# A four-layer decoder trunk on one core: scaled activations and split weights at staggered SBUF addresses, and two gate/up tiles multiplied in pieces

## The chip, the core and the metric

One core of one Trainium2 chip runs the whole trunk in one launch. The metric is the device time of that core in microseconds (us), taken as the median over runs. The host only permutes and joins the arrays that it is given.

## What is computed

Two layers of a macaron block. Each adds half a SwiGLU feed-forward, then a mixer (differential attention in layer 0, a chunked gating MLP in layer 1), then half of another feed-forward. All of it is float32.

```python
D_MODEL = 1024; SEQ = 512; D_FF = 2816
def _swiglu_ffn(x, w_gate_up, w_down):
    g, u = jnp.split(x @ w_gate_up, 2, axis=-1)
    return (jax.nn.silu(g) * u) @ w_down
def reference(...):
    for i in range(2):
        x = x + 0.5 * _swiglu_ffn(_rmsnorm(x, ffn1_norm[i]), ffn1_w_gate_up[i], ffn1_w_down[i])
        h = _rmsnorm(x, mix_norm[i])
        x = x + (_diff_attention(h, ...) if i == 0 else _chunked_sgu(h, ...))
        x = x + 0.5 * _swiglu_ffn(_rmsnorm(x, ffn2_norm[i]), ffn2_w_gate_up[i], ffn2_w_down[i])
    return x
```

## The kernel before

The residual lies on chip as eight tiles `x[k]`, 128 features by 512 tokens each. A product of float32 operands is made of three products of float32r operands (a float32 format that TensorE multiplies in one pass): each operand is split into a high part and the remainder, and `mm3` (lines 126 to 129) adds high times high, high times low and low times high in PSUM. One such matmul has 128 stationary columns (a piece of one operand, 512 bytes of each partition) and 512 moving columns (2048 bytes of each partition of the other operand). The TensorE row of a trace that belongs to it is MATMUL; the load of its stationary part is a LDWEIGHTS on the row PEld. The load for the next matmul starts when the present matmul starts.

- **Scaled x.** `Norm.halves` (lines 156 to 159) writes x times gain as `xh[k]` on ScalarE and its remainder `xl[k]` on VectorE, eight tiles of 2048 bytes each.
- **Weights.** `load` (line 113) brings up to 2048 columns into a raw tile through the SP queue; `split` (lines 118 to 124) makes a high and a low tile of up to 1024 columns from a part of it, out of a pool of five buffers for each. Weights are split ahead of their use.
- **Feed-forward** (`ffn`, f0 to f3, in the order of the trunk). 22 gate/up tiles of 48 matmuls: the weights are stationary and `xh`/`xl` move; then 16 down tiles of 33 matmuls: weights stationary, hidden tiles `hh`/`hl` moving. Each half of the hidden width does 11 gate/up tiles and 8 down tiles. f0 is the first of layer 0, f1 the second of layer 0. Down products are called `f0dp` to `f3dp` in rows, gate/up products `f0p` to `f3p`.
- **Attention** (`qk`, `v`, `aop` in rows) and **gating MLP** (`gv`, `gup`, `gs`, `gop`). In their input products (`qk`, `v`, `gv`) a piece of `xh`/`xl` is stationary and the weights move. `interleave` (line 311) emits the tasks of a mixer in the order of a rough clock. In the gating MLP: `v_block` (the columns mixed over tokens, `gv`), `layer_norm` and `affine` (four pairs of VectorE operations for each block of 512 columns, lines 692 and 693), `u_tile` (24 matmuls each, `gup`, kept in tiles `gut`), `mix` (four float32 matmuls, `gs`, line 707, that need the block's affine), and `out_part` (`gop`, with the mixed tiles `gh`/`gl` moving). `U_BUFS = 4` is the number of `gut` buffers, and u tile c is emitted only after mix c - U_BUFS.

Where the operands stand in SBUF, in bytes within a partition, as the built program places them (the trace does not show addresses):

```text
operand                          first byte      spacing   remainder by 512
xh[k], xl[k]                     36960           2048      96
split weights (pieces of 512 B)  69728 onwards   512       96
hidden tiles hh, hl              137440          2048      224
mixed tiles gh, gl               193152          2048      128
```

So in all products of x with weights, and in the attention's output product, the moving tile and the stationary piece begin at the same remainder by 512 bytes. In the down products they differ by 128 bytes, in the gating MLP's output products by 32.

Of the kernel before, what the change touches and what calls it, by code (L numbers as in the profile page):

```python
# [10 lines left out]
F32R = mybir.dt.float32r  # L11
# [6 lines left out]
P = 128  # L18
S = 512
NT = S // P  # L20
D = 1024
KT = D // P
# [22 lines left out]
O_BUFS = 4  # L45
U_BUFS = 4
QK_BUFS = 5
BANKS = {"pp": 4, "ps": 3, "po": 1}
HOP = 0.2
END = "end"  # L50


@with_exitstack
def kernel(
# [18 lines left out]
):  # L73
    """Activations stay on chip. The residual is kept feature-major, x[d, token]; float32 operands
    of the large products are split exactly into a float32r part and its float32r remainder, and
    hi*hi + hi*lo + lo*hi accumulate in PSUM. The RMS factor of a token is applied where a
    product leaves PSUM, so that products start on x*gain before it is known."""
    nc = tc.nc

    const = ctx.enter_context(tc.tile_pool(name="const", bufs=1))  # L80
    acts = ctx.enter_context(tc.tile_pool(name="acts", bufs=1))
    wraw = ctx.enter_context(tc.tile_pool(name="wraw", bufs=2))
    wsplit = ctx.enter_context(tc.tile_pool(name="wsplit", bufs=5))
# [7 lines left out]
    x = [acts.tile([P, S], F32, name=f"x{k}") for k in range(KT)]  # L91
    xh = [acts.tile([P, S], F32R, name=f"xh{k}") for k in range(KT)]
    xl = [acts.tile([P, S], F32R, name=f"xl{k}") for k in range(KT)]
    ident = const.tile([P, P], F32, name="ident")
# [16 lines left out]

# [1 line left out]
    def load(src, n, name):  # L113
# [4 lines left out]
    def split(raw, lo, n, name):  # L118
        """Exact float32r halves of n columns of raw."""
        wh = wsplit.tile([P, 1024], F32R, tag="wh", name=name + "h")  # L120
        wl = wsplit.tile([P, 1024], F32R, tag="wl", name=name + "l")
        nc.scalar.activation(wh[:, :n], raw[:, lo:lo + n], AF.Copy)
        nc.vector.tensor_tensor(wl[:, :n], raw[:, lo:lo + n], f32(wh[:, :n]), op=ALU.subtract)
        return wh, wl

    def mm3(ps, sh, sl, mh, ml, start, stop):
        nc.tensor.matmul(ps, sh, mh, start=start, stop=False)  # L127
        nc.tensor.matmul(ps, sh, ml, start=False, stop=False)  # L128
        nc.tensor.matmul(ps, sl, mh, start=False, stop=stop)  # L129

    def rsqrt(v, n, name):
        """v ** -0.5 of a [P, n] tile, to float32 rounding."""
        y = stat.tile([P, n], F32, tag=f"rs_y{n}", name=name + "y")
        t = stat.tile([P, n], F32, tag=f"rs_t{n}", name=name + "t")
        nc.vector.tensor_scalar(
            y.bitcast(I32), v.bitcast(I32), -0.5, RSQRT_MAGIC, op0=ALU.mult, op1=ALU.add
        )
        for _ in range(3):
            nc.vector.tensor_tensor(t, y, y, op=ALU.mult)
            nc.vector.scalar_tensor_tensor(t, t, -0.5, v, op0=ALU.mult, op1=ALU.mult)  # L140
            nc.vector.scalar_tensor_tensor(y, t, 1.5, y, op0=ALU.add, op1=ALU.mult)
        return y

    class Norm:
        """Collects x*gain and the sum of squares of a new residual, tile by tile."""

# [22 lines left out]
        def rstd(self):  # L169
            """[token, token tile] of 1/rms."""  # L170
            ps = bank(self.name + "ss", "po")
            for n in range(NT):
                nc.tensor.matmul(
                    ps[:, n:n + 1], self.acc[:, n * P:(n + 1) * P], ones[:, 0:1], start=True, stop=True
                )
            v = stat.tile([P, NT], F32, tag="rs_v4", name=self.name + "v")
            nc.vector.tensor_scalar(v, ps[:, :NT], 1.0 / D, RMS_EPS, op0=ALU.mult, op1=ALU.add)
            return rsqrt(v, NT, self.name)

        def rows(self, r):  # L180
            """[any partition, token] of 1/rms."""
            rh = stat.tile([P, NT], F32R, tag="rh", name=self.name + "rh")
            rl = stat.tile([P, NT], F32, tag="rl", name=self.name + "rl")
            nc.vector.tensor_scalar(rh, r, 1.0, None, op0=ALU.mult)
            nc.vector.tensor_tensor(rl, r, f32(rh), op=ALU.subtract)
            ps = bank(self.name + "rb", "po")
            for part, half in ((f32(rh), "h"), (rl, "l")):
                dg = stat.tile([P, NT, P], F32R, tag="sq", name=f"{self.name}dg{half}")
                nc.vector.tensor_tensor(
                    dg,  # L190
                    ident.unsqueeze(1).broadcast_to([P, NT, P]),
                    part.unsqueeze(2).broadcast_to([P, NT, P]),
                    op=ALU.mult,
                )
                nc.tensor.matmul(
                    ps, ones_r, dg.rearrange("p a b -> p (a b)"), start=(half == "h"), stop=(half == "l")
                )
            rb = stat.tile([P, S], F32, tag="rb", name=self.name + "rbs", bufs=1)
            nc.scalar.activation(rb, ps, AF.Copy)
            return rb  # L200

    def begin(norm):
        """Loads of x and of the first weights, in the order of their use, and their halves."""
        raw = wraw.tile([P, 2048], F32, tag="raw", name="w0")
        cuts = [(0, 1), (1, 2), (2, 4), (4, 6), (6, 8)]
        for a, b in cuts:
# [3 lines left out]
        nc.sync.dma_start(sm[:, C_BOUT:], small[:, C_BOUT:])  # L210
        parts = [
            [wsplit.tile([P, 1024], F32R, tag=t, name=f"w0{q}{t}") for t in ("wh", "wl")] for q in range(2)
        ]
        for a, b in cuts:
# [11 lines left out]
    def ffn(layer, which, norm, nxt):  # L226
        f = layer * 2 + which
        nm = f"f{f}"
        with ExitStack() as c:
# [19 lines left out]
            for half in range(2):  # L249
                hh, hl, late = [], [], []  # L250
                for jj in range(FH):
# [7 lines left out]
                    for k in range(KT):  # L259
                        wh, wl = parts[k // 4]  # L260
                        for u in range(2):
                            c0 = slice((k % 4 * 2 + u) * P, (k % 4 * 2 + u + 1) * P)
                            mm3(ps[u], wh[:, c0], wl[:, c0], xh[k], xl[k], k == 0, k == KT - 1)
                        if rb is None and jj == first:
                            if k == 3:
                                r = norm.rstd()
                            elif k == KT - 1:
                                rb = norm.rows(r)
# [23 lines left out]
    class Weights:  # L292
        """Pieces of 1024 columns of weights in the order of their use, two to a load, split ahead of it."""

# [16 lines left out]
    def interleave(tasks):  # L311
        """Emits tasks in the order of a rough clock of the engines. A task is (name, names of the
        tasks whose results it needs, or "<" and names of those that it only follows, generator); the
        generator yields (products' share, shares of the engines that take up the result one after the
        other, whether it waits for them or until when, or END); the earlier in the list, the higher
        its priority."""
        done, state, sent, now = {}, {}, {}, 0.0
# [36 lines left out]
    def project(weights, p, nm, norm, rr, taken):  # L354
        """[token, 512 columns] of x*gain against four pieces, p on, of weights; taken() emits what
        takes a token tile out of PSUM and returns the engines' shares."""
        ps = [bank(f"{nm}p{n}", "pp") for n in range(NT)]
# [21 lines left out]
    def attention(norm, nxt):  # L379
        with ExitStack() as c:  # L380
            a2 = c.enter_context(tc.tile_pool(name="a2", bufs=2, reuse_waits="tile"))

            # k gain * q gain / sqrt(d) on k; (1 - lambda_init) * subln gain; -lambda
            kg = const.tile([P, 1], F32, name="kg")
# [27 lines left out]
            def qk_block(hp):  # L412
                """q and k of two heads."""
                nm = f"qk{hp}"
# [12 lines left out]
            def v_block(b):  # L427
                """v of four heads."""
                vts[b] = a2.tile([P, NT, 512], F32, tag="vt", name=f"vt{b}", bufs=2)
# [48 lines left out]
            def scores(h, i):  # L478
                """Both softmaxes of query tile i, each before its division, and their difference."""
                hp, hh, nm = h // 2, h % 2, f"a{h}"  # L480
# [133 lines left out]
    def gmlp(norm, nxt):  # L614
        with ExitStack() as c:
# [34 lines left out]
            def v_block(b):  # L650
                """gelu of the 512 columns that are mixed over tokens."""
                br = row(b_in, 4 + b, "bin")
# [10 lines left out]
            def u_tile(c):  # L663
                """gelu of a tile of gates, [column, token]."""
                if "rb" not in rr:
# [30 lines left out]
            def mix(c):  # L696
                """Mixes a tile of v over the tokens of each chunk, [column, token], and gates it."""
                b, j, g = c // 4, c % 4, c // 2
# [60 lines left out]

# [1 line left out]
    nc.sync.dma_start(sm[:, :C_BOUT], small[:, :C_BOUT])  # L761
# [84 lines left out]
```

## Time and profile before

| | |
|---|---|
| time, median of 2 runs | 2024.37 us (2024.16 and 2024.58) |
| span of the profiled execution | 2022.6 us; the runs' time lies 1.8 us above it |
| TensorE matmul / weight load | 2012.6 us (100%) / 1627.5 us (80%) |
| VectorE / ScalarE / GpSimd | 1026.9 us (51%) / 670.4 us (33%) / 2.6 us |
| DMA | 190.33 MB, 26.7% of 16 engines for the data queue |
| granted TensorE clock, mean | 1.000 |

Busy times of matmuls overlap, since one starts while the one before it drains. The distance between the starts of neighbouring matmuls, called the pitch below, is what a matmul costs, and not its duration of 0.39 us. A row of the timeline has the start, the duration, the engine, the line, and output<-inputs.

### The profile page before, as it was taken

What the parts mean: (1) busy time and instruction counts of PE and PEld (TensorE: products, weight loads), DVE (VectorE), ACT (ScalarE), POOL (GpSimd) and SP (SyncE); (2) the same over time, 40 slices, a digit from 0 to 9 for tenths busy, and PEclk for the clock granted to TensorE, in tenths of its full rate; (3) what the DMA queues carried; (4) which work ended last, traced back from release to release, by engine and by line L of the source; (5) the groups of instructions that cost most, each with busy time, mean ns of one, the idle gap of its engine ahead of it and who ended that gap; (6) DMA issues with size and microseconds to landing.
All of it is one profiled execution on the core that took longest, in us unless ns stands there. A gap on an engine that the chain in (4) does not pass through costs nothing.

```text
span 2022.6 us, 22047 instructions
## 1 busy us (share of the span) xinstructions
PE 2012.6 (100%) x8970; PEld 1627.5 (80%) x8970; DVE 1026.9 (51%) x1647; ACT 670.4 (33%) x960; POOL 2.6 (0%) x11
## 2 busy tenths in 40 slices
PE   8999999999999999999999999999999999999999
PEld 7888888876668888888888888888888888888887
DVE  7433444556768543444454334444596564434442
ACT  5322323355554322232332223233332243222321
POOL 0000000000000000000000000000000000000000
PEclk9999999999999999999999999999999999999999
DMA  5223222211111222222322232224332222223222
GB/s 190 98 72 124 92 85 93 105 63 63 42 63 64 105 85 92 105 104 72 108 102 91 78 115 102 79 99 146 115 115 84 85 103 85 84 93 124 84 80 77
DMA packets 32933, 190.33 MB, mean 94 GB/s; under 512 B 3776, under 2 KB 4160, under 8 KB 16576
## 3 DMA queue, kind: packets, MB, share of 16 engines
q1 hardware_dynamic: 32832, 188.93, 26.7%
q8 instruction: 70, 1.15, 0.2%
q14 instruction: 31, 0.25, 0.0%
HBM read 186.82 MB, written 2.10 MB: 93 GB/s over the span
## 4 chain that ended last, share of the span: by engine, by line
PE 99%; DVE 0%; DMA 0%; ACT 0%; SPq 0%; issue 0%
PE f3p L127 4%; PE f2p L127 4%; PE f2p L128 4%; PE f3p L128 4%; PE f2p L129 4%; PE f3p L129 4%; PE f1p L128 4%; PE f1p L129 4%; PE f1p L127 4%; PE f0p L127 4%; PE f0p L129 4%; PE f0p L128 4%; PE f1dp L129 2%; PE f0dp L127 2%; PE f1dp L128 2%; PE f0dp L128 2%
## 5 line engine op out<-in xcount | busy, mean ns | idle before, releaser
L235 DVE TENSOR_TENSOR f3g<-f3p,n5rbs 128x512 f32<-128x512 f32 x22 | 15.2, 691 | 58.7 <-PE f3p L129 58.7
L235 DVE TENSOR_TENSOR f2g<-f2p,n3rbs 128x512 f32<-128x512 f32 x22 | 15.2, 691 | 58.7 <-PE f2p L129 58.7
L235 DVE TENSOR_TENSOR f1g<-f1p,n2rbs 128x512 f32<-128x512 f32 x22 | 15.2, 692 | 58.7 <-PE f1p L129 57.3
L235 DVE TENSOR_TENSOR f0g<-f0p,n0rbs 128x512 f32<-128x512 f32 x22 | 15.2, 691 | 55.5 <-PE f0p L129 55.5
L158 ACT ACTIVATE xh<-x,sm 128x512 fp32r<-128x512 f32 x48 | 34.3, 718 | 18.0 <-DVE x L737 9.5
L159 DVE SCALAR_TENSOR_TENSOR xl<-x,sm,xh 128x512 fp32r<-128x512 f32 x48 | 35.6, 746 | 8.6 <-ACT xh L158 8.5
L285 DVE SCALAR_TENSOR_TENSOR x<-f3dp,x 128x512 f32<-128x512 f32 x16 | 11.1, 692 | 42.3 <-PE f3dp L129 42.3
L491 PEld LDWEIGHTS <-ident_b 128*128 128x128 bf16 x64 | 6.1, 95 | 28.1 <-issue 26.2
L285 DVE SCALAR_TENSOR_TENSOR x<-f1dp,x 128x512 f32<-128x512 f32 x16 | 11.1, 692 | 31.0 <-PE f1dp L129 31.0
L285 DVE SCALAR_TENSOR_TENSOR x<-f2dp,x 128x512 f32<-128x512 f32 x16 | 11.1, 692 | 31.0 <-PE f2dp L129 31.0
L285 DVE SCALAR_TENSOR_TENSOR x<-f0dp,x 128x512 f32<-128x512 f32 x16 | 11.1, 692 | 31.0 <-PE f0dp L129 31.0
L737 DVE TENSOR_TENSOR x<-gop,x 128x512 f32<-128x512 f32 x24 | 16.5, 689 | 19.8 <-PE gop L129 19.8
L242 ACT ACTIVATE f3hh<-f3u 128x512 fp32r<-128x512 f32 x22 | 13.9, 632 | 28.0 <-DVE f3u L239 28.0
L242 ACT ACTIVATE f2hh<-f2u 128x512 fp32r<-128x512 f32 x22 | 13.9, 632 | 28.0 <-DVE f2u L239 28.0
L243 DVE TENSOR_TENSOR f3hl<-f3u,f3hh 128x512 fp32r<-128x512 f32 x22 | 15.2, 693 | 15.4 <-ACT f3hh L242 15.4
L243 DVE TENSOR_TENSOR f2hl<-f2u,f2hh 128x512 fp32r<-128x512 f32 x22 | 15.2, 693 | 15.4 <-ACT f2hh L242 15.4
L242 ACT ACTIVATE f1hh<-f1u 128x512 fp32r<-128x512 f32 x22 | 13.9, 631 | 27.2 <-DVE f1u L239 27.2
L580 DVE TENSOR_TENSOR x<-aop,x 128x512 f32<-128x512 f32 x32 | 21.4, 684 | 2.8 <-PE aop L129 2.7
L243 DVE TENSOR_TENSOR f1hl<-f1u,f1hh 128x512 fp32r<-128x512 f32 x22 | 15.2, 692 | 14.7 <-ACT f1hh L242 14.7
L242 ACT ACTIVATE f0hh<-f0u 128x512 fp32r<-128x512 f32 x22 | 13.9, 632 | 26.4 <-DVE f0u L239 26.4
L243 DVE TENSOR_TENSOR f0hl<-f0u,f0hh 128x512 fp32r<-128x512 f32 x22 | 15.2, 692 | 14.1 <-ACT f0hh L242 14.0
L717 ACT ACTIVATE gh<-gut 128x512 fp32r<-128x512 f32 x16 | 10.1, 631 | 33.8 <-DVE gut L716 33.8
(3603 smaller groups left out, 6451.7 us busy)
## 6 DMA issues: line engine op xcount, KB each, us to landing
f1gu<-in_gate_up_dram SPq DMA_DIRECT2D x22, 1024.0 KB, 4.8
f2gu<-in_gate_up_dram SPq DMA_DIRECT2D x22, 1024.0 KB, 4.7
f3gu<-in_gate_up_dram SPq DMA_DIRECT2D x22, 1024.0 KB, 4.8
f0gu<-in_gate_up_dram SPq DMA_DIRECT2D x21, 1024.0 KB, 4.8
f0d<-in_down_dram SPq DMA_DIRECT2D x16, 704.0 KB, 4.0
f1d<-in_down_dram SPq DMA_DIRECT2D x16, 704.0 KB, 4.1
f2d<-in_down_dram SPq DMA_DIRECT2D x16, 704.0 KB, 4.0
f3d<-in_down_dram SPq DMA_DIRECT2D x16, 704.0 KB, 4.0
```

Of the source, the lines that this page charges most:

```text
L127: nc.tensor.matmul(ps, sh, mh, start=start, stop=False)
L128: nc.tensor.matmul(ps, sh, ml, start=False, stop=False)
L129: nc.tensor.matmul(ps, sl, mh, start=False, stop=stop)
L158: nc.scalar.activation(xh[k], x[k], AF.Copy, scale=g)
L159: nc.vector.scalar_tensor_tensor(xl[k], x[k], g, f32(xh[k]), op0=ALU.mult, op1=ALU.subtract)
L235: nc.vector.tensor_tensor(gt, ps[0], rb, op=ALU.mult)
L242: nc.scalar.activation(a, ut, AF.Copy)
L243: nc.vector.tensor_tensor(b, ut, f32(a), op=ALU.subtract)
L285: nc.vector.scalar_tensor_tensor(x[m], pt, 0.5, x[m], op0=ALU.mult, op1=ALU.add)
L580: nc.vector.tensor_tensor(x[m], pt, x[m], op=ALU.add)
L717: nc.scalar.activation(gh, ut, AF.Copy)
L737: nc.vector.tensor_tensor(x[m], pt, x[m], op=ALU.add)
```

## The change

Three things. First, `xh[k]`, `xl[k]` and each split tile get 192 bytes more, and the operand begins at 0 to 6 steps of 32 bytes inside its tile: k mod 7 steps for `xh[k]`, 3k+4 mod 7 for `xl[k]`, and for the q-th pair of split tiles q mod 7 and 3q + q//8 mod 7. Second, to make room, `U_BUFS` is 2. Third, in f1 the gate/up tiles 3 and 5 take their moving operand in two pieces of 256 columns and four pieces of 128 columns, and the stationary part is loaded anew for each matmul of a piece.

```diff
-U_BUFS = 4
+U_BUFS = 2
+SHIFT = 8
+PAD = 6 * SHIFT
...
-    xh = [acts.tile([P, S], F32R, name=f"xh{k}") for k in range(KT)]
-    xl = [acts.tile([P, S], F32R, name=f"xl{k}") for k in range(KT)]
+    def shifted(pool, n, at, name, **kw):
+        o = at % 7 * SHIFT
+        return pool.tile([P, n + PAD], F32R, name=name, **kw)[:, o:o + n]
+    xh = [shifted(acts, S, k, f"xh{k}") for k in range(KT)]
+    xl = [shifted(acts, S, 3 * k + 4, f"xl{k}") for k in range(KT)]
+    places = iter(range(1 << 20))
+    def halves_of(name):
+        q = next(places)
+        return shifted(wsplit, 1024, q, name + "h", tag="wh"), shifted(wsplit, 1024, 3 * q + q // 8, name + "l", tag="wl")
...
-        wh = wsplit.tile([P, 1024], F32R, tag="wh", name=name + "h")
-        wl = wsplit.tile([P, 1024], F32R, tag="wl", name=name + "l")
+        wh, wl = halves_of(name)
...
-    def mm3(ps, sh, sl, mh, ml, start, stop):
+    def mm3(ps, sh, sl, mh, ml, start, stop, cuts=1):
+        if cuts > 1:
+            n = S // cuts
+            for a in range(0, S, n):
+                c = slice(a, a + n)
+                nc.tensor.matmul(ps[:, c], sh, mh[:, c], start=start and a == 0, stop=False)
+                nc.tensor.matmul(ps[:, c], sh, ml[:, c], start=False, stop=False)
+                nc.tensor.matmul(ps[:, c], sl, mh[:, c], start=False, stop=stop and a + n == S)
+            return
...
-                            mm3(ps[u], wh[:, c0], wl[:, c0], xh[k], xl[k], k == 0, k == KT - 1)
+                            cuts = {(1, 3): 2, (1, 5): 4}.get((f, j), 1)
+                            mm3(ps[u], wh[:, c0], wl[:, c0], xh[k], xl[k], k == 0, k == KT - 1, cuts)
```

In the built program after it `xh[k]` stands 2240 bytes apart, the split tiles 4288 bytes apart, and the shift comes on top. The hidden tiles begin at remainder 96 and the mixed tiles at 0. The remainder by 256 of (moving minus next stationary) then takes all eight multiples of 32 about equally often: among f1's 1248 gate/up matmuls each of the eight comes 124 to 170 times, among its 528 down matmuls 27 to 88 times.

On TensorE the first place is f1's gate/up tile 3 (`f1w30h` and `f1w30l` are the high and low parts of its first weights; `f1p_5349` and `f1p_5350` are the gate and the up accumulator). Before:

```order
L127 MATMUL f1p_5349<-xh_82,f1w30h 128x512
L128 MATMUL f1p_5349<-xl_90,f1w30h 128x512
L129 MATMUL f1p_5349<-xh_82,f1w30l 128x512
L127 MATMUL f1p_5350<-xh_82,f1w30h 128x512
L128 MATMUL f1p_5350<-xl_90,f1w30h 128x512
L129 MATMUL f1p_5350<-xh_82,f1w30l 128x512
```

With the change, the three rows of each accumulator come twice with 256 columns (shown once here):

```order
L144 MATMUL f1p_5349<-xh_82,f1w30h 128x256
L145 MATMUL f1p_5349<-xl_90,f1w30h 128x256
L146 MATMUL f1p_5349<-xh_82,f1w30l 128x256
...
L144 MATMUL f1p_5350<-xh_82,f1w30h 128x256
L145 MATMUL f1p_5350<-xl_90,f1w30h 128x256
L146 MATMUL f1p_5350<-xh_82,f1w30l 128x256
```

Tile 5 reads the same with four groups of 128x128. TensorE has 8858 rows where it had 8666: 48 more in tile 3, 144 more in tile 5.

On TensorE the second place is the first mix of the gating MLP (`gup` is the product of a u tile, `gs` that of a mix, and `gv_9780` to `gv_9783` are the four token tiles that `affine` finishes on VectorE). Before, the mixes of the first block come after all of u tile 3:

```order
L127 MATMUL gup_10494<-xh_89,gu2s1h 128x512
L128 MATMUL gup_10494<-xl_97,gu2s1h 128x512
L129 MATMUL gup_10494<-xh_89,gu2s1l 128x512
L707 MATMUL gs_10530<-wT,gv_9780 128x128
L707 MATMUL gs_10530<-wT,gv_9781 128x128
```

With the change (the token tiles are now `gv_9972` on) two mixes stand within u tile 2, after 13 of its matmuls:

```order
L150 MATMUL gup_10682<-xh_85,gu2s0l 128x512
L148 MATMUL gup_10682<-xh_86,gu2s0h 128x512
L727 MATMUL gs_10656<-wT,gv_9972 128x128
L727 MATMUL gs_10666<-wT,gv_9972 128x128
L149 MATMUL gup_10682<-xl_94,gu2s0h 128x512
L727 MATMUL gs_10656<-wT,gv_9973 128x128
L727 MATMUL gs_10666<-wT,gv_9973 128x128
L150 MATMUL gup_10682<-xh_86,gu2s0l 128x512
```

So 61 matmuls of u tiles stand ahead of the first mix, where there were 96.

On VectorE, at the same place, the first affine operation that a mix needs (line 693 before, line 713 now) stood right behind the rows of the next block:

```order
L692 SCALAR_TENSOR_TENSOR gv_9782<-gv_9782,lnmv,lng_10570 128x512
L693 SCALAR_TENSOR_TENSOR gv_9780<-gv_9780,lny,lnb_10452 128x512
L676 TENSOR_TENSOR gut_10447<-gup_10422,n4rbs 128x512
L693 SCALAR_TENSOR_TENSOR gv_9781<-gv_9781,lny,lnb_10452 128x512
```

With the change the take-up of u tile 1 and a split of weights stand ahead of it:

```order
L696 TENSOR_TENSOR gut_10639<-gup_10614,n4rbs 128x512
L162 SCALAR_TENSOR_TENSOR lny<-lnt,lny 128x4
L136 TENSOR_TENSOR gu6s0l<-gu6r,gu6s0h 128x1024
L713 SCALAR_TENSOR_TENSOR gv_9972<-gv_9972,lny,lnb_10644 128x512
L713 SCALAR_TENSOR_TENSOR gv_9973<-gv_9973,lny,lnb_10644 128x512
```

In the rest of the gating MLP mixes, u tiles and the loads and splits between them shift in the same manner, on SP, ScalarE, VectorE and TensorE; the mixes come in 17 groups on TensorE, where there were 9. Outside it the order of the engines is the same, but for one pair of neighbours on VectorE and ScalarE behind tile 5 of f1.

## Rows read from the trace of the kernel before

**Rows 1.** The page: busy time by engine, granted clock, the chain by engine.
```profile
PE 2012.6 (100%) x8970; PEld 1627.5 (80%) x8970; DVE 1026.9 (51%) x1647; ACT 670.4 (33%) x960; POOL 2.6 (0%) x11
...
PEclk9999999999999999999999999999999999999999
...
PE 99%; DVE 0%; DMA 0%; ACT 0%; SPq 0%; issue 0%
```

**Rows 2.** Waits of TensorE: us in total, times, longest us.
```profile
PE f0p L127 <- ACT w00wh L218: 5.8, 2, 5.2
PE f0p L127 <- ACT f0w10h L122: 0.2, 1, 0.2
PE n2rb L195 <- DVE n2dgh L189: 0.2, 1, 0.2
```

**Rows 3.** Timeline of PE in f1's gate/up tiles, first and last of 51.
```profile
899.62 0.39 PE L127 MATMUL f1p<-xh,f1w170h 128*128 128x512 f32 x1
899.85 0.39 PE L128 MATMUL f1p<-xl,f1w170h 128*128 128x512 f32 x1
...
910.95 0.39 PE L129 MATMUL f1p<-xh,f1w180l 128*128 128x512 f32 x1
```

**Rows 4.** Timeline of PE in f1's down tiles, first and last of 48.
```profile
773.80 0.39 PE L128 MATMUL f1dp<-f1hl,f1dw00bh 128*128 128x512 f32 x1
774.03 0.40 PE L129 MATMUL f1dp<-f1hh,f1dw00bl 128*128 128x512 f32 x1
774.27 0.39 PE L127 MATMUL f1dp<-f1hh,f1dw00bh 128*128 128x512 f32 x1
774.50 0.40 PE L128 MATMUL f1dp<-f1hl,f1dw00bh 128*128 128x512 f32 x1
...
784.77 0.40 PE L127 MATMUL f1dp<-f1hh,f1dw02ah 128*128 128x512 f32 x1
```

**Rows 5.** Timeline of PE in the gating MLP's output product, first and last of 49.
```profile
1639.64 0.40 PE L129 MATMUL gop<-gh,gw30s1l 128*128 128x512 f32 x1
...
1650.84 0.40 PE L129 MATMUL gop<-gh,gw31s1l 128*128 128x512 f32 x1
```

**Rows 6.** Timeline of PE in f2's gate/up tile 1, behind two other matmuls.
```profile
1022.93 0.39 PE L195 MATMUL n3rb<-n3dgl,ones_r 128*128 128x512 f32 x1
1023.16 0.40 PE L127 MATMUL f2p<-xh,f2w10h 128*128 128x512 f32 x1
1023.40 0.40 PE L128 MATMUL f2p<-xl,f2w10h 128*128 128x512 f32 x1
...
1025.24 0.39 PE L127 MATMUL f2p<-xh,f2w10h 128*128 128x512 f32 x1
1025.47 0.39 PE L128 MATMUL f2p<-xl,f2w10h 128*128 128x512 f32 x1
1025.69 0.39 PE L129 MATMUL f2p<-xh,f2w10l 128*128 128x512 f32 x1
```

**Rows 7.** Timeline of PE: the first mixes and the u tile behind them.
```profile
1486.74 2.17 PE L707 MATMUL gs<-wT,gv 128*128 128x128 f32 x18
1488.67 0.48 PE L127 MATMUL gup<-xh,gu4s0h 128*128 128x512 f32 x1
1488.99 0.40 PE L128 MATMUL gup<-xl,gu4s0h 128*128 128x512 f32 x1
```

**Rows 8.** Instructions of line 707 and of tile f1p: ns min/median/max, first and last start.
```profile
L707 PE MATMUL gs<-wT,gv x128: 270/275/275, 1485.2 to 1615.3; 128*128 128x128 f32 x128
...
L127 PEld LDWEIGHTS f1p<-xh,f1w00h x8: 187/187/188, 646.2 to 651.0; 128*128 128x128 f32 x8
```

**Rows 9.** Timeline of the gating MLP: first u tile on PE, then VectorE.
```profile
1463.38 0.40 PE L127 MATMUL gup<-xh,gu0s0h 128*128 128x512 f32 x1
...
1474.83 0.75 DVE L693 SCALAR_TENSOR_TENSOR gv<-gv,lny,lnb 128x512 f32<-128x512 f32 x1
1475.49 0.68 DVE L676 TENSOR_TENSOR gut<-gup,n4rbs 128x512 f32<-128x512 f32 x1
1476.10 2.07 DVE L693 SCALAR_TENSOR_TENSOR gv<-gv,lny,lnb 128x512 f32<-128x512 f32 x3
1478.08 1.22 DVE L123 TENSOR_TENSOR gu6s0l<-gu6r,gu6s0h 128x1024 fp32r<-128x1024 f32 x1
```

More of the change, by code (lines that the diff above doesn't have):

```diff
@@ L210, in begin @@
         nc.sync.dma_start(sm[:, C_BOUT:], small[:, C_BOUT:])
-        parts = [
-            [wsplit.tile([P, 1024], F32R, tag=t, name=f"w0{q}{t}") for t in ("wh", "wl")] for q in range(2)
-        ]
+        parts = [halves_of(f"w0{q}w") for q in range(2)]
         for a, b in cuts:
```

## The prediction

> **What bounds the kernel.** I read the page first: TensorE is busy for 100% of the span, VectorE for 51%, ScalarE for 33%, the chain that ended last is TensorE to 99%, and the granted clock stands at its full level in every slice [rows 1]. TensorE waits 6.2 us in all, nearly all of it once at the start [rows 2]. So only what changes the cost of a matmul, or makes TensorE wait anew, can move the time. The clock can't explain differences between stages: it is the same in all.
>
> Then I read the pitch (the distance between starts) stage by stage from the timeline. In gate/up, 50 pitches take 910.95 - 899.62 = 11.33 us, or 226.6 ns each [rows 3]. In the down products, 47 pitches take 784.77 - 773.80 = 10.97 us, or 233.4 ns [rows 4]. In the gating MLP's output product 48 pitches take 11.20 us, or 233.3 ns [rows 5]. The shape is the same in all three, 128 stationary and 512 moving columns, and no row shows TensorE waiting there. What differs is where the operands stand: in the first case the moving tile and the next stationary piece begin at the same remainder by 512 bytes, in the second they differ by 128 bytes, in the third by 32. Accumulating in one or two PSUM banks is not the reason, since the weight-times-x products of the gating MLP keep one bank for 24 matmuls as the output product keeps one for 12, and gate/up changes it after three.
>
> A second thing: behind two other matmuls, nine pitches of gate/up take 1025.24 - 1023.16 = 2.08 us, 231 ns each, with neighbours of 0.23 and 0.24 us [rows 6]; only then does the pitch fall to 0.22 to 0.23 us and stay. So 226.6 ns is a state that a stream at one constant address difference settles into after about nine matmuls, and before that it costs what the other two stages cost, within 2 ns.
>
> **The change, part by part.**
>
> *The addresses.* After the change the difference between the moving tile and the next stationary piece varies from matmul to matmul over eight values, so no nine neighbours in a row have the same one. I expect the stream never to settle. Its price is bounded by rows: below by 226.6 ns (it settles all the same), above by the longer of the alternating pitches in rows 4, 0.24 us. Rows of down and output products say 233.3, the unsettled stretch of gate/up says 231. I take 232, between these, since the latter is nearest to what the change makes. How many matmuls pay it? Of equal remainder there are 4 x 22 x 48 = 4224 in gate/up, 576 in the attention's q, k and v, 192 in its output, 384 and 384 in the gating MLP's v and u: 5760. I leave out the 96 of the two cut tiles and half of the attention's 768, which are broken up by short matmuls and so unsettled already: 5280. 5280 x (232 - 226.6) ns = +28.5 us. The 4 x 528 down and 384 output products lose their fixed difference too: 2496 x (232 - 233.3) ns = -3.2 us. Together +25.3 us. All of it is on the path, since TensorE has no slack.
>
> The shifts cost ScalarE, VectorE and the DMA nothing that I can price: counts, shapes and bytes are the same, and a slower TensorE gives them more cover; at half load [rows 1] they have room.
>
> *Tile 3 of f1, two pieces.* 96 matmuls of 256 columns for 48 of 512. Half of 226.6 is 113.3 ns; a 128-column load in a stream that is nothing but loads and short matmuls comes every 111.8 ns: (2.17 - 0.27) us over 17 pitches [rows 7, 8]. So the pitch is at least 113 ns. If what 226.6 has over twice the bare streaming belongs to each load and not to each column, it comes to about 123; I take that. 96 x 0.123 - 48 x 0.2266 = 11.8 - 10.9 = +0.9 us. At 113 ns it would cost nothing.
>
> *Tile 5 of f1, four pieces.* 192 matmuls of 128 columns. A quarter of 226.6 is 57 ns, so the load sets the pitch, and each of the 192 has one. The nearest row is the same 111.8 ns, although of float32 operands. 192 x 0.1118 - 10.9 = 21.5 - 10.9 = +10.6 us. From above: if the shown 187 ns of a load [rows 8] were its full price, 35.9 - 10.9 = +25.0 us; but in rows 7 a load of that very duration comes every 111.8 ns. From below, at 57 ns, nothing.
>
> The Trainium skill bears on this term ("TensorE: Matmul & The Clock Gate", Back-to-back issue gap): a stream of pairs of load and matmul with 128 columns is said to sustain about 81 ns a matmul. By that the tile would cost 192 x 0.081 - 10.9 = +4.7 us; rows 7 speak against it for four-byte operands.
>
> *The gating MLP with two u buffers.* Mixes need the affine of their block, and 61 matmuls now stand ahead of the first, not 96. TensorE would reach it at 1463.38 + 61 x 0.232 = 1477.5 us on the clock of before [rows 9]. On VectorE the affine operations began at 1474.83 and ended at 1478.17, with a 0.68 us take-up between them; now that take-up and a 1.22 us split stand ahead of all four, so they would run from about 1477.1 to 1479.8 us. TensorE then waits about half a us for the first token tile and a few tenths for the next; behind the waiting mix all of TensorE is queued. Mixes are also scattered more: they come in 17 groups rather than 9, and each return to long matmuls costs 0.32 rather than 0.23 us [rows 7], 8 x 0.09 = 0.7 us. On the SP queue some loads of the affine's rows change places with their neighbours, without one being added. Together +2 us; 0 if VectorE is early, 5 if later blocks are late as well.
>
> **Sum.** 25.3 + 0.9 + 10.6 + 2 = +38.8 us on a span of 2022.6: 2061.4. The runs' median lies 1.8 us above the span, so 2063 us, 1.9% more than 2024.37. About 2% is what a measurement of this kernel can tell from no change, and that bound stands at 2064.9, so the forecast lies just inside it.
>
> **Rivals.**
>
> *It locks into a longer pitch (slower by more than 2%).* The change moves each load off the moving tile's remainder, and if each odd difference costs what 128 or 32 bytes cost now, every product pays 233.3 to 234 ns or more. At 234: 5280 x 7.4 + 2496 x 0.7 ns = 39.1 + 1.7, with 13.5 for the rest +54 us: 2079. At 237, which the longer half of rows 4 comes near (0.24 us at the printed digits), it is +78 us: 2102. The 2% bound is crossed from a mean pitch of 232.2 ns on. For it: both constant differences that rows show cost 233.3. Against: the mean over changing ones need not be that of a fixed one.
>
> *Addresses don't matter (slower, within 2%).* Load and moving stream don't meet, and the 6.7 ns between rows 3 and rows 4 have another cause, for instance that the hidden tiles lie elsewhere in SBUF. Then only pieces and buffers cost: +13.5 us, 2038. For it: VectorE and ScalarE write into the same memory all the time and leave gate/up's pitch alone. Against: rows 6 show 231 ns with the same `xh` and `xl` that rows 3 stream at 226.6.
> The Trainium skill states this rule ("TensorE: Matmul & The Clock Gate", Step-by-step: what each phase is for): TensorE reads through two independent ports, and loading the next weights takes nothing from the running matmul. Rows 3 to 5 do not settle it: a pitch that depends on the stage doesn't follow from the rule, but does not refute it either.
>
> *Spreading removes conflicts (not slower).* If equal remainders are the bad case in part, and some differences that no row shows are better, the mean falls. No group of rows has a mean under 226; at 224 ns, which I put 2.6 ns below the best group, it gives 5280 x (-2.6) + 2496 x (-9.3) ns = -37 us, and +13.5: 2001 us. It decides once the mean over all these products is under 227.0 ns (2496 x 6.3 - 5280 x 0.4 ns = 13.6 us less, as much as pieces and buffers cost): the kernel is then not slower. Faster by more than 2% it is only from 221.8 on. For it: of three cases I know one that is good and two that are not, and five differences are unseen. Against: the good one is the equal one, which the change gives up.
>
> **How the numbers follow.** Forecast 0.52: a mean pitch of 231 to 233, which is 2055 to 2071 us (+30.9 to +46.5), 0.30 of it within 2% and 0.22 above. Longer pitch 0.15, all slower. Addresses don't matter 0.18, within 2%. Spreading helps 0.15, of that 0.05 faster by over 2%. Sums: faster 0.05, same 0.30 + 0.18 + 0.10 = 0.58, slower 0.22 + 0.15 = 0.37. The time is that of the forecast, 2063. The range takes in the no-effect case below, with a few us for cheaper pieces (2032), and 234.5 ns with dear ones above (2084).
>
> **What would show it.** In the profile after: gate/up starts 231 to 233 ns apart and irregular, with no long stretch at 226.6; down at 231 to 233 rather than an alternation of two; tile 3 of f1 lasting about 11.8 us and tile 5 about 21.5 us; two short waits of TensorE at line 727 under 3 us. The forecast is wrong if gate/up still stands at 226.6, if its mean is over 234 or under 230, or if tile 5 takes over 25 us.

## The result and the profile after

The kernel with the change takes 2059.51 us (median of two runs, 2059.41 and 2059.60) where the kernel before takes 2024.37: a ratio of 1.0173, 95% interval 1.0154 to 1.0192. It is slower by 1.7%, 3.5 us less than forecast. The span of the profiled execution is 2057.7 us, 35.1 us more than before.

The page after the change, with the same lines as in [rows 1]:

```profile
PE 2047.8 (100%) x9162; PEld 1642.9 (80%) x9162; DVE 1028.7 (50%) x1647; ACT 669.8 (33%) x960; POOL 2.6 (0%) x11
...
PEclk9999999999999999999999999999999999999999
...
PE 99%; DMA 0%; SPq 0%; ACT 0%; DVE 0%; issue 0%
```

TensorE is still all that bounds the kernel, and the granted clock is full in every slice, as before. So the 35 us are neither a wait nor a clock: the same matmuls cost more, and the two cut tiles have 192 more of them. The view of waits has one line left for TensorE, the one at the start, as in [rows 2]; none has come at line 727, the mixes:

```profile
PE f0p L148 <- ACT w00wh L237: 5.9, 2, 5.2
```

The timeline of TensorE (start, duration, engine, line, output<-inputs) over the 51 gate/up matmuls of f1 that [rows 3] showed, first and last:

```profile
916.03 0.39 PE L148 MATMUL f1p<-xh,f1w170h 128*128 128x512 f32 x1
916.26 0.40 PE L149 MATMUL f1p<-xl,f1w170h 128*128 128x512 f32 x1
...
927.64 0.39 PE L150 MATMUL f1p<-xh,f1w180l 128*128 128x512 f32 x1
```

50 pitches take 11.61 us, 232.2 ns each, where they took 226.6. The 49 output-product matmuls of [rows 5], in the same view, first and last:

```profile
1662.69 0.39 PE L148 MATMUL gop<-gh,gw30s0h 128*128 128x512 f32 x1
...
1673.84 0.39 PE L148 MATMUL gop<-gh,gw31s0h 128*128 128x512 f32 x1
```

48 pitches in 11.15 us: 232.3 ns, where they took 233.3. So both kinds of product have moved to the same 232, one up and the other down. In every stage the mean of the undisturbed pitches now lies between 231.5 and 232.6 ns.

The two cut tiles, in the timeline: tile 3 from its first row to tile 4's first row, tile 5 from its first to tile 6's first.

```profile
688.33 0.28 PE L144 MATMUL f1p<-xh,f1w30h 128*128 128x256 f32 x1
688.45 0.28 PE L145 MATMUL f1p<-xl,f1w30h 128*128 128x256 f32 x1
...
699.57 0.28 PE L146 MATMUL f1p<-xh,f1w31l 128*128 128x256 f32 x1
699.69 0.39 PE L148 MATMUL f1p<-xh,f1w40h 128*128 128x512 f32 x1
...
710.85 0.22 PE L144 MATMUL f1p<-xh,f1w50h 128*128 128x128 f32 x1
710.91 0.27 PE L145 MATMUL f1p<-xl,f1w50h 128*128 128x128 f32 x1
711.02 0.28 PE L146 MATMUL f1p<-xh,f1w50l 128*128 128x128 f32 x1
...
732.12 0.28 PE L146 MATMUL f1p<-xh,f1w51l 128*128 128x128 f32 x1
732.24 0.44 PE L148 MATMUL f1p<-xh,f1w60h 128*128 128x512 f32 x1
```

Tile 3 takes 699.69 - 688.33 = 11.36 us, 118.3 ns for each matmul of 256 columns. Tile 4, uncut, takes 11.16. Tile 5 takes 732.24 - 710.85 = 21.39 us: 191 pitches in 21.27 us, 111.4 ns each.

### The profile page after: what moved, and what is told of

It is laid out like the page before. It is cut to its first block, busy times and chain, and to the rows that moved or that the text cites. A ratio compares the mean times of both kernels' runs of the same rounds, so it can differ in the third digit from the quotient of the medians.

```text
span 2057.7 us, 22436 instructions
## 1 busy us (share of the span) xinstructions
PE 2047.8 (100%) x9162; PEld 1642.9 (80%) x9162; DVE 1028.7 (50%) x1647; ACT 669.8 (33%) x960; POOL 2.6 (0%) x11
## 4 chain that ended last, share of the span: by engine, by line
PE 99%; DMA 0%; SPq 0%; ACT 0%; DVE 0%; issue 0%
PE f2p L148 4%; PE f2p L149 4%; PE f3p L148 4%; PE f3p L149 4%; PE f2p L150 4%; PE f3p L150 4%; PE f0p L148 4%; PE f0p L150 4%; PE f0p L149 4%; PE f1p L148 4%; PE f1p L149 4%; PE f1p L150 4%; PE f2dp L148 2%; PE f1dp L148 2%; PE f3dp L150 2%; PE f3dp L149 2%
```

## The experiments

Two theories stood at the start. A: the distance between starts depends on where the moving tile stands against the stationary piece, and a mix of differences averages 232. B: addresses are nothing to the pitch; the pieces and the two u buffers cost what is lost. All runs stand beside runs of the kernel before on the same chip; the times of that kernel lay between 2024.41 and 2025.35 us. The pieces and the addresses were each run twice and the kernel with all differences at zero four times; the other times are of single executions, and what they show rests on the pitches in their traces.

**Pieces and two u buffers alone.**

```diff
 kernel before, with
-U_BUFS = 4
+U_BUFS = 2
+                            cuts = {(1, 3): 2, (1, 5): 4}.get((f, j), 1)
```

> The kernel before with the two cut tiles and two u buffers, all addresses as before. Theory A (the pitch of a matmul hangs on the distance between the address of its moving tile and that of the stationary piece loaded beside it): gate/up stays at 226.6 ns, tile 3 of f1 takes 11.4 us and tile 5 21.4 us as in the changed kernel, 2024.4 + 0.5 + 10.5 = 2035 us. Theory B (addresses do nothing, pieces and buffers cost it all): 2059 us, as the changed kernel.

It took 2035.9 us, 1.0054 (1.0034 to 1.0074) of the kernel before: A's number. Its timeline at tiles 3 and 5, at the first u tile of the gating MLP and at the first matmul of f3:

```profile
680.75 0.28 PE L131 MATMUL f1p<-xh,f1w30h 128*128 128x256 f32 x1
...
692.14 0.28 PE L133 MATMUL f1p<-xh,f1w31l 128*128 128x256 f32 x1
...
703.17 0.22 PE L131 MATMUL f1p<-xh,f1w50h 128*128 128x128 f32 x1
...
724.45 0.28 PE L133 MATMUL f1p<-xh,f1w51l 128*128 128x128 f32 x1
...
1474.48 0.40 PE L135 MATMUL gup<-xh,gu0s0h 128*128 128x512 f32 x1
...
1666.22 0.39 PE L135 MATMUL f3p<-xh,f3w00h 128*128 128x512 f32 x1
```

Tile 5: 191 pitches in 21.28 us, 111.4 ns, the same as with spread addresses: with 128 columns it changes nothing where the operands stand. That the load sets this pitch, and not the moving columns, shows in the kernel before, where eight matmuls with a load of 128 columns each have a single moving column (count, ns min/median/max, first and last start, shape):

```profile
L173 PEld LDWEIGHTS n1ss<-ones,n1acc x8: 188/192/192, 388.8 to 389.7; 128*128 128x128 f32 x8
L173 PE MATMUL n1ss<-ones,n1acc x8: 164/250/250, 389.1 to 389.8; 128*128 128x1 f32 x8
```

From their starts in ns, the second to the last of them stand 111.7 ns apart too. Tile 3: 95 pitches in 11.39 us, 119.9 ns, here a little more than with spread addresses (118.3). From the first u tile to f3 it takes 1666.22 - 1474.48 = 191.74 us. In the kernel before that stretch began at 1463.38 [rows 9] and ended with this row:

```profile
1654.58 0.39 PE L127 MATMUL f3p<-xh,f3w00h 128*128 128x512 f32 x1
```

That is 191.20 us. So two u buffers cost about 0.5 us, all told.

**Addresses alone.**

```diff
 kernel after, with
-                            cuts = {(1, 3): 2, (1, 5): 4}.get((f, j), 1)
+                            cuts = 1
```

> The changed kernel without the pieces (addresses and two u buffers alone). Theory A: every product stays at a mean pitch of 232.0 ns, 2059.5 - 11.0 = 2048.5 us. Theory B: 2024 us.

2049.1 us, 1.0119 (1.0099 to 1.0139): A again, and B's 2024 is out. Beside the 2024.87 us that the kernel before took with these runs (a median of seven), addresses and buffers cost 24.2 us, pieces and buffers 11.0. With the 0.5 of the buffers counted once the parts add up to 34.7; the change as a whole cost 35.1.

**A sweep of constant differences.** The split weights are moved by another step for each weight tile, so that all 48 (33) matmuls of a tile have one difference.

```diff
 kernel before, U_BUFS = 2, with
-        wh = wsplit.tile([P, 1024], F32R, tag="wh", name=name + "h")
+        wh = wsplit.tile([P, 1152], F32R, tag="wh", name=name + "h")[:, at:at + 1024]
...
+                        at = ((f - 1) * FT + j) % 64 if f else 0
+                    at = 2 * (16 * f + 8 * half + m)
```

The same for `wl`; `at` counts 4-byte words.

> The kernel before with each weight tile shifted by an offset that is constant within a gate/up or down tile: 4-byte steps from 0 to 252 over the 66 gate/up tiles of f1 to f3 (the last two are 0 and 4 again), 8-byte steps from 0 to 504 over all 64 down tiles; f0's gate/up is not shifted. Theory A1 (any constant distance settles, changing ones do not): most tiles settle near 226.6 or 233.3, mean in gate/up under 230 ns, time 2020 to 2030 us. Theory A2 (each distance has a price of its own and 232.0 is their mean): the tiles of one distance differ from each other by several ns and their mean is 232, 3168 x 5.4 ns more in gate/up and 2112 x 1.4 ns less in down: 2038 us. Theory B: all gate/up tiles at 226.6 and all down tiles at 233.3, 2024 us.

2039.0 us, the value of A2: a constant difference does not settle at 226.6 ns, it settles at a price of its own. Four gate/up tiles of f3 in its timeline, first and last of 48 matmuls each; the differences by 256 are 64, 44, 32 and 28 bytes:

```profile
1710.70 0.39 PE L127 MATMUL f3p<-xh,f3w40h 128*128 128x512 f32 x1
...
1721.45 0.40 PE L129 MATMUL f3p<-xh,f3w41l 128*128 128x512 f32 x1
...
1766.39 0.39 PE L127 MATMUL f3p<-xh,f3w90h 128*128 128x512 f32 x1
...
1777.49 0.40 PE L129 MATMUL f3p<-xh,f3w91l 128*128 128x512 f32 x1
...
1861.30 0.40 PE L127 MATMUL f3p<-xh,f3w120h 128*128 128x512 f32 x1
...
1872.27 0.39 PE L129 MATMUL f3p<-xh,f3w121l 128*128 128x512 f32 x1
1872.49 0.39 PE L127 MATMUL f3p<-xh,f3w130h 128*128 128x512 f32 x1
...
1883.15 0.40 PE L129 MATMUL f3p<-xh,f3w131l 128*128 128x512 f32 x1
```

47 pitches take 10.75, 11.10, 10.97 and 10.66 us. From the starts in ns, without the first nine pitches of each tile, the steady prices are these (0 is from f0, the others from one tile each):

```text
difference by 256, bytes   0     28    32    44    64    92    96    128   136   160   192   224
ns a matmul              226.7 226.7 233.3 236.7 228.9 236.8 233.4 233.3 226.7 234.4 233.3 233.3
```

Nothing lies under 226.65 ns, nothing over 236.84, five tiles aside that are broken by a pitch of about 0.8 us or more. Each price is a mean: away from the floor the pitches of a tile repeat a pattern, at 92 bytes 229, 234, 257, 237 and 230 ns over and over, at 44 bytes 234 and 239 in turn, though all matmuls of the tile have the same difference. The down products of the same run give the same value at the same difference in nearly all cases (64: 228.9, 136: 226.7, 160: 234.3). Two don't fit: a difference of 112 costs 226.7 ns in gate/up (first and last of 48) and 233.4 in a down tile (first and last of 33),

```profile
145.62 0.39 PE L127 MATMUL f0dp<-f0hh,f0dw02ah 128*128 128x512 f32 x1
...
153.09 0.39 PE L129 MATMUL f0dp<-f0hh,f0dw02bl 128*128 128x512 f32 x1
...
1234.39 0.39 PE L127 MATMUL f2p<-xh,f2w140h 128*128 128x512 f32 x1
...
1245.05 0.40 PE L129 MATMUL f2p<-xh,f2w141l 128*128 128x512 f32 x1
```

7.47 us over 32 pitches and 10.66 over 47; and one down tile at 40 bytes took 226.7 ns where another tile at 40 took 232.1. So the price is not a function of the difference by 256 alone. The eight multiples of 32 have a mean of 232.1 ns, and the change's mix of them pays 232. That the mix pays the mean of these prices is not shown: the runs further down find mixes that don't.

**All differences at zero.** Two gaps move the hidden tiles and the mixed tiles to the weights' remainder.

```diff
 kernel before, with
+            nc.gpsimd.memset(hp.tile([P, 96], F32, tag="gap", name=nm + "gap"), 0.0)
+            nc.gpsimd.memset(ap.tile([P, 120], F32, name="ggap"), 0.0)
```

> The kernel before with a gap of 384 bytes ahead of the hidden tiles and one of 480 bytes ahead of the mixed tiles, so that these begin at the weights' remainder by 512 as the scaled x does. Theory A: down and output products fall from 233.3 to 226.6 ns, 2496 x 6.7 ns = 16.7 us less: 2007.7 us. Theory B: 2024 us, down products at 233.3 as before.

2008.47 us, 0.9919 (0.9902 to 0.9936): 16.4 us less than the kernel before, where A gives 2496 x (233.3 - 226.67) ns = 16.5 us. Its timeline in the first down tile (33 matmuls) and in an output tile (48), first and last:

```profile
764.24 0.39 PE L127 MATMUL f1dp<-f1hh,f1dw00ah 128*128 128x512 f32 x1
...
771.50 0.39 PE L129 MATMUL f1dp<-f1hh,f1dw00bl 128*128 128x512 f32 x1
...
1620.05 0.39 PE L127 MATMUL gop<-gh,gw30s0h 128*128 128x512 f32 x1
...
1630.71 0.39 PE L129 MATMUL gop<-gh,gw30s1l 128*128 128x512 f32 x1
```

7.26 us over 32 pitches and 10.66 over 47: 226.8 ns each, where [rows 4] and [rows 5] have 233.4 and 233.3. Of what TensorE reads there, only the address of the moving operand has changed.

**All addresses moved alike.**

```diff
 kernel before, with
+    nc.gpsimd.memset(acts.tile([P, 5], F32, name="ahead"), 0.0)
     xh = [acts.tile([P, S], F32R, name=f"xh{k}") for k in range(KT)]
```

> The kernel before with a tile of 20 bytes ahead of the scaled x, so that x, weights, hidden and mixed tiles all stand 20 bytes further on and every difference is kept. If only the difference between moving tile and next piece counts: 2024.9 us, gate/up at 226.7 and down at 233.3 ns. If the absolute address of one of them counts (an edge that x now straddles): gate/up at another pitch, and by the spread of the sweep up to 10 ns x 5500 = +55 us.

In the built program the tile of 20 bytes takes 32, so the shift is one of 32 bytes, and a shift of less is not tested. The run took 2025.0 us beside 2024.54, with gate/up at 226.8 and down at 233.3 ns. The start of f1's gate/up tile 17, and its last matmul:

```profile
894.98 0.39 PE L128 MATMUL f1p<-xh,f1w170h 128*128 128x512 f32 x1
...
905.63 0.39 PE L130 MATMUL f1p<-xh,f1w171l 128*128 128x512 f32 x1
```

47 pitches in 10.65 us, 226.6 ns. The sweep moved the weights by the same 32 bytes without x (224 in its table), and that cost 233.3 ns. So a shift of all operands by 32 bytes is nothing; where they stand to each other is what counts.

**Which difference?** The load for the next matmul runs beside the present one (N), but the present matmul's own piece could count as well (O), or each matmul could pay the steady price of its difference (P), or a change of difference could cost by itself (V). The first run moves `xl` and `wl` by 32 bytes, so that every moving tile is level with the next piece.

```diff
 kernel before, U_BUFS = 2, with
-    xl = [acts.tile([P, S], F32R, name=f"xl{k}") for k in range(KT)]
+    xl = [acts.tile([P, S + 64], F32R, name=f"xl{k}")[:, 8:8 + S] for k in range(KT)]
...
-        wl = wsplit.tile([P, 1024], F32R, tag="wl", name=name + "l")
+        wl = wsplit.tile([P, 1088], F32R, tag="wl", name=name + "l")[:, 8:8 + 1024]
```

> The kernel before with xl and the low weight tiles both 32 bytes further on, two u buffers. In gate/up each moving tile then begins at the same remainder by 256 as the piece that is loaded beside it (the next one), but against its own piece, loaded before it, the differences are 0, 32 and -32 bytes in turn. Theory N (the load that runs beside the moving stream counts): gate/up stays at 226.7 ns and the time at 2025 us within 3. Theory O (the matmul's own piece counts): the mean of the steady prices at 0, 32 and 224 in the sweep, (226.7 + 233.3 + 233.3)/3 = 231.1 ns in gate/up, q, k, v, gv and gup, 5472 x 4.4 ns = +24 us, 2049 us.

2053.74 us, gate/up at 232.2 ns. The same tile 17, first and last:

```profile
907.38 0.40 PE L127 MATMUL f1p<-xh,f1w170h 128*128 128x512 f32 x1
...
918.29 0.39 PE L129 MATMUL f1p<-xh,f1w171l 128*128 128x512 f32 x1
```

47 pitches in 10.91 us. N is out: to be level with the next piece is not enough. O's 231.1 is nearer, and misses by 1.1 ns.

The next keeps those tiles and multiplies other pairs, so that every moving tile is level with its own piece:

```diff
 kernel of the run above, with
-        nc.tensor.matmul(ps, sh, ml, start=False, stop=False)
-        nc.tensor.matmul(ps, sl, mh, start=False, stop=stop)
+        nc.tensor.matmul(ps, sh, mh, start=False, stop=False)
+        nc.tensor.matmul(ps, sl, ml, start=False, stop=stop)
```

> The kernel of the pair run (xl and low weight tiles both 32 bytes further on) with other products: the second matmul of three takes xh again in place of xl, the third takes xl in place of xh, so the computation is changed there and the counts and shapes are not. In gate/up each moving tile is then level with its own stationary piece always, and against the next piece the differences are 0, 224 and 32 in turn. Theory O (own piece counts): 226.7 ns in gate/up, some 2025 us. Theory N (next piece counts): 231 ns or more in gate/up. Theory S (the whole sequence of moving and stationary remainders counts, and only products that are level throughout keep the floor): 231 to 237 ns, 2049 to 2080 us, and no other arrangement with a 32-byte step in it at 226.7 either.

2053.29 us, gate/up at 232.2 ns, in tile 17:

```profile
907.11 0.40 PE L127 MATMUL f1p<-xh,f1w170h 128*128 128x512 f32 x1
...
918.03 0.39 PE L129 MATMUL f1p<-xl,f1w171l 128*128 128x512 f32 x1
```

47 pitches in 10.92 us. O is out too. What is left of the three (N, O and S in the expectation) is S, that the whole sequence of remainders counts.

The weights' low tiles alone, by 120 and by 32 bytes:

```diff
 kernel before, U_BUFS = 2, with
-        wl = wsplit.tile([P, 1024], F32R, tag="wl", name=name + "l")
+        wl = wsplit.tile([P, 1152], F32R, tag="wl", name=name + "l")[:, 30:30 + 1024]
```

> The kernel before with only the low weight tiles moved, by 120 bytes, two u buffers. Against the next piece the differences in gate/up are 0, 136, 0 in turn, and both were at the floor of 226.7 ns when the sweep held them. Theory P (each matmul pays the steady price of its own difference): gate/up stays at 226.7 ns. Theory V (a change of difference from matmul to matmul costs by itself, whatever the differences): gate/up at 229 to 233 ns. The down products have differences of 128 and 8 in turn, both at 233.3 in the sweep: P keeps them at 233.3, V leaves them between 230 and 235. The gate/up products alone decide: P about 2025 us, V 2037 to 2057 us.

2023.34 us, with gate/up at 226.7 to 226.8 ns, in tile 17:

```profile
894.94 0.39 PE L127 MATMUL f1p<-xh,f1w170h 128*128 128x512 f32 x1
...
905.59 0.39 PE L129 MATMUL f1p<-xh,f1w171l 128*128 128x512 f32 x1
```

47 pitches in 10.65 us. A change between these two differences, both at the floor, costs nothing, so V is out in its plain form. The down products, though, fell to 231.1 ns from differences (128 and 8) that each cost 233.3 when constant, and P had them stay. The products of weights with x (q, k, v, gv), whose differences there are 0 and 120, rose to between 231 and 233.4 ns, which is why the time is not lower still.

For 32 bytes the same edit with `1088` and `8:8 + 1024`:

> The kernel before with only the low weight tiles moved, by 32 bytes, two u buffers: differences against the next piece of 0, 224, 0 in turn in gate/up. Theory P (steady price of each difference, added up): (226.7 + 233.3 + 226.7)/3 = 228.9 ns in gate/up, 4224 x 2.2 = +9.4 us and some 2 us in the attention and the gating MLP, 2036 us. Theory V (the change itself costs): 231 to 233 ns, 4224 x 4.4 to 6.4 = +19 to +27 us, 2045 to 2055 us.

2057.89 us, dearer than either theory had it. In its timeline the start of f1's gate/up tile 17, and its last matmul:

```profile
909.17 0.40 PE L127 MATMUL f1p<-xh,f1w170h 128*128 128x512 f32 x1
...
920.15 0.39 PE L129 MATMUL f1p<-xh,f1w171l 128*128 128x512 f32 x1
```

47 pitches in 10.98 us, 233.6 ns here and 233.3 over all of gate/up. Sorted by place in the group of three, over f2's gate/up, the means are 232.5 ns behind (high, high), 238.8 behind (high, low x), whose next piece is the moved one, and 228.5 behind (low, high), with a scatter of about 1 ns. P's sum for them is 226.7 + 233.3 + 226.7. So the prices of constant differences can't be added up. The first of the three has a moving tile that is level with its own piece and with the next one, and is still followed by 232.5 ns and not 226.7: own and next piece together don't settle the price, and something of the matmuls around it counts as well.

**One spread at a time.** x alone and the weights alone, without pieces, with two u buffers:

```diff
 kernel after, cuts = 1; x alone:
-        return shifted(wsplit, 1024, q, name + "h", tag="wh"), shifted(wsplit, 1024, 3 * q + q // 8, name + "l", tag="wl")
+        return wsplit.tile([P, 1024], F32R, tag="wh", name=name + "h"), wsplit.tile([P, 1024], F32R, tag="wl", name=name + "l")
 the weights alone:
-    xh = [shifted(acts, S, k, f"xh{k}") for k in range(KT)]
+    xh = [acts.tile([P, S], F32R, name=f"xh{k}") for k in range(KT)]
```

The second has the same line for `xl`.

> The spread of scaled x alone (weights at 96 by 512 as before, no pieces, two u buffers): in gate/up, q, k, v, gv and gup the differences change with k and between high and low, down and output products keep 128 and 32. Theory mean price: 231.5 to 232.5 ns in the former, 233.3 in the latter, 5568 x (232 - 227) ns = +28 us, 2053 us. If each spread brought a share of the loss: about half of +24, 2037 us.

> The spread of the split weights alone (scaled x as before, no pieces, two u buffers): the differences change with the weight tile and between high and low, in the down products too. Theory mean price: 231.5 to 232.5 ns in every product, the same 2049 us as with both spreads. If each spread brought a share of the loss: about half of it, 2037 us.

2047.91 us for x alone, 2049.86 for the weights alone. Each spread by itself costs, within 1.3 us, what both cost together (2049.1); shares are out. x alone has gate/up at 231.1 ns, a ns less than I expected, with down and output products at 233.3 as before; the weights alone give 231.9 to 232.3 in gate/up and down.

## Why the prediction was right, and where its steps were not

- *What bounds it.* Right: TensorE before and after, at full clock. The two short waits foretold at line 727 are not in the view of waits.
- *The addresses, +25.3 us from a mean pitch of 232 ns.* Right in both halves: gate/up went from 226.6 up to 232.2, the output product from 233.3 down to 232.3, and the addresses alone cost 24.2 - 0.5 = 23.7 us.
- *The reason given for it* was wrong in one step: "226.6 ns is a state that a stream at one constant address difference settles into". The sweep shows that a constant difference settles too, but mostly higher, up to 236.8 ns; zero is one of a few that reach the floor. [rows 4] and [rows 5] had shown this already: down and output products do have constant differences and stand at 233.3. The forecast held because I put the mix between the unsettled stretch of [rows 6] and these two, and 232 lies there. So the size is in part luck: no step of the prediction says why a mix should cost 232, and the runs don't either.
- *Tile 5, +10.6 us.* Right: 21.39 - 10.88 = +10.5, from a load-bound pitch of 111.4 ns, which the mixes' 111.8 [rows 7] had foretold although their operands are float32. 10.88 us is 48 x 226.6 ns.
- *Tile 3, +0.9 us.* Right in sign, its size 0.4 us off: 11.36 - 10.88 = +0.5. The term took 123 ns a matmul, by way of a bare streaming time that no row gives; 118.3 was measured.
- *Two u buffers, +2 us.* Mis-sized: 0.5 us in the run of pieces and buffers. I let TensorE wait at the first mix. After the change VectorE does begin the affine late, behind the split, in its timeline:

```profile
1504.64 1.23 DVE L136 TENSOR_TENSOR gu6s0l<-gu6r,gu6s0h 128x1024 fp32r<-128x1024 f32 x1
1505.78 2.73 DVE L713 SCALAR_TENSOR_TENSOR gv<-gv,lny,lnb 128x512 f32<-128x512 f32 x4
```

while TensorE comes to the first mix with this:

```profile
1506.31 0.40 PE L148 MATMUL gup<-xh,gu2s0h 128*128 128x512 f32 x1
1506.67 0.68 PE L727 MATMUL gs<-wT,gv 128*128 128x128 f32 x4
1507.11 0.48 PE L149 MATMUL gup<-xl,gu2s0h 128*128 128x512 f32 x1
1507.42 0.61 PE L727 MATMUL gs<-wT,gv 128*128 128x128 f32 x4
```

  The first of the four affine operations would end near 1506.5 us, at a quarter of 2.73, and the mix starts at 1506.67, 0.36 us behind the matmul before it. So the order was as foreseen, but the lateness about 0.1 us and not 0.5; and between the mixes stands a long matmul in which the next operation catches up.
- *The sum.* +38.8 forecast, +35.1 measured; 1.5 of the 3.7 us between them is the u buffers' term, 0.4 tile 3, 0.1 tile 5, and the 1.7 left over is the addresses', which alone came 1.6 us under their 25.3.
- *The rivals.* "Addresses don't matter" fell by the zero-difference run and by the addresses alone. The Trainium skill's rule beside it ("TensorE: Matmul & The Clock Gate", Step-by-step: what each phase is for), that loading the next weights takes no SBUF read bandwidth from the running matmul, does not agree with these runs for float32r operands, if it is read as the rival reads it: 226.7 or 233.3 ns for the same matmuls, by the address of one operand. Bandwidth itself was not measured. "Spreading removes conflicts" fell: no constant difference went under 226.65 ns. "Longer pitch" is true of single differences (44 and 92 bytes) and of the run with low tiles moved by 32 bytes, and wrong for the mean of this change's mix. Its premise was nearly true: six of the seven multiples of 32 other than zero cost 233.3 ns or more when constant, and only 64 bytes is cheaper.
- The Trainium skill's figure of about 81 ns a matmul at 128 columns ("TensorE: Matmul & The Clock Gate", Back-to-back issue gap) does not agree with tile 5: 111.4 ns.

Open stays why a difference has the price it has, and what exactly a matmul carries over to the next. The runs rule out the next piece alone, the own piece alone, both together, the sum of constant prices, and a flat charge for every change.

## What to carry to other kernels

When TensorE is busy throughout and the same shape has two pitches in two stages, look at where its operands stand: here moving tiles and stationary pieces at one remainder by 256 bytes gave the lowest pitch in every product of 512 moving columns, and two small gaps in the layout were worth 16.4 us (0.8%). Steps between tiles meant to spread them cost 24 us instead, and a spread of one operand alone costs about as much as of both. Pieces of 128 columns nearly double a tile's time (21.39 us for 10.88) when the stationary part is loaded anew for each, since the load then sets the pitch.

## What was not expected of the hardware

The pitch of one and the same matmul, 128 by 512 in float32r, ran from 226.65 to 236.84 ns by the relative address of its operands in steps as small as 4 bytes (28 bytes 226.7, 32 bytes 233.3, 44 bytes 236.7), within one execution at a granted clock of 1.000. Single matmuls in a repeating group of three stood at 238.8 and 228.5 ns side by side. And with 256 columns level operands were not the best: 119.9 ns a matmul with all differences at zero, 118.3 with the spread ones; I did not look into that further.
